# First expert gather of a layer from a contiguous copy of h, and new holds of the weight ring

## The chip, the cores and the metric

The kernel runs on one core of a Trainium2 chip. The metric is the device time of one execution in microseconds, the median of several runs. TensorE (PE; its weight loads are listed apart, as PEld), VectorE (DVE), ScalarE (ACT), GpSimd (POOL) and SyncE (SP, which issues the weight DMAs) run side by side and wait for each other by semaphores.

## The reference

Two layers of a decoder trunk over 256 tokens with 1024 features, in float32. Layer 0 mixes tokens by a gated short convolution and stick-breaking attention (the even mixer), layer 1 by a chunked gMLP (the odd mixer). After the mixer each layer has a mixture of experts: a router picks one of four groups and two of the group's eight experts for each token. Then comes a gate with a per-layer embedding, and a final norm.

```python
for i in range(DEPTH):
    xn = rmsnorm(h, norm_mix[i])
    h = h + (even_mixer if i % 2 == 0 else odd_mixer)(xn, ...)
    xn = rmsnorm(h, norm_ffn[i])
    h = h + hier_moe(xn, router_c[i], ..., moe_w1[i], moe_w3[i], moe_w2[i])
    gate = jax.nn.sigmoid(rmsnorm(h, norm_pl[i]) @ w_pg[i])
    h = h + gate * (p[i] @ w_pe[i])
return rmsnorm(h, final_norm)
# hier_moe, for each expert e of 32, width 256:
#   y += comb[:, e] * ((silu(xt @ w1[e]) * (xt @ w3[e])) @ w2[e])
```

## The kernel before, in words

**Storage.** h lies in SBUF with the tokens on the partitions: `h[P, 2, 1024]`, two tiles of 128 tokens. The view `hk` takes feature p*8+k as [k, p], so that `hk[:, tt, k, :]` is 128 features that lie eight floats apart; the experts' weights are loaded with the same order of features (`(p k) n -> p k n`), which gives long pieces in DRAM.

**The ring.** All large tiles and all weights share one pool of 25 buffers of one megabyte (`rawp`, `big`). `emit_loads` (L107) issues the next weight load while the live raw loads, two for each split unit, one for the load itself, one spare and `pos["hold"]` fit into 25. `HOLD` and `MOE_HOLD` are lists of holds, set at fixed places of the program, and keep room for the other large tiles of that stage. Weights are loaded in the order of use, by SP alone; a load is queued on SP in program order and waits there until the last reader of its buffer is done.

**The order of work.** It is written out by hand. In `odd_mixer` (L680) eight output units are interleaved with the projections and the gates (`gate`, L717): gate i+1 comes ahead of output unit i. `finish_mixer` (L463) does the last output unit, adds to h, turns h by TensorE into `hT` (L458), and computes the router's logits (L473) and 40 small matmuls on a tile of ones (L498). `moe` (L785) ranks the logits on VectorE and makes from them the selection matrix `S` of the first group (L849). `gather` (L855) multiplies: for each of eight k, `hk[:, tt, k, :]` is the weight and S the moving operand, so that the tokens of each expert stand in columns (`xg`); the result leaves PSUM through VectorE (L866). The first gather of a layer takes 128 columns of the first group (four experts with 32 places each), in two calls of four k. Then, for each quarter of a group, `up` (L910) multiplies by w1 and w3 of four experts and gives back their four buffers (`drop_raw`, L187, which calls `emit_loads`), and `down` (L962) does the same with w2. The second half of the first group is gathered after the first quarter's up-projections, the further groups whole, after every second quarter.

**What the change touches.** The two lists of holds (L31, L32), the end of `finish_mixer`, the loop over the output units in `odd_mixer` (L746 to L757), the weight operand of `gather` (L863), the place after the first two gathers (L872), and what hands the new tile through (L675, L758, L785, L1253 to L1287).

Of the kernel before, what the change touches and what calls it, by code (L numbers as in the profile page):

```python
# [15 lines left out]
P = 128  # L16
T = 256
D = 1024
KD = 8
# [8 lines left out]
NEG = -1.0e30  # L28
BUFS = 25
SPARE = 1  # L30
HOLD = (9, 2, 9, 8, 8, 6, 8)  # L31
MOE_HOLD = (0, 5, 10, 6, 1, 0)  # L32
UP_PIECES = 2
DOWN_PIECES = 2
MIX_PIECES = 1
# [11 lines left out]
def body(tc, x, p, norm_mix, norm_ffn, norm_pl, final_norm,  # L47
# [4 lines left out]
    nc = tc.nc  # L52
# [11 lines left out]
    def psum(name, tag="mm", dt=F32):  # L64
        n = 1024 if tag == "y" else 512
        return pp.tile([P, n], dt, name=name, tag=tag)

    def big(name, shape, dt=F32):
        return rawp.tile(shape, dt, name=name, tag="raw")
# [26 lines left out]
    pos = {"load": 0, "split": 0, "take": 0, "hold": HOLD[0]}  # L96
# [168 lines left out]
    h = cp.tile([P, 2, D], F32, name="h")  # L265
# [190 lines left out]
    def turn_plain(tt, n, hT):  # L456
        tv = turned(tt, n)
        nc.scalar.copy(hT[:, 4 * n:4 * n + 4, tt * P:(tt + 1) * P], tv)  # L458


    hk = h.rearrange("t a (p k) -> t a k p", k=KD)

    def finish_mixer(li, ops, ys, nxt, wr):  # L463

        pos["hold"] = MOE_HOLD[0]
        g = cols[:, FFN_C + 8 * li:FFN_C + 8 * li + 8].unsqueeze(2).to_broadcast([P, KD, 36])
        nc.vector.tensor_tensor(wr, wr, g, op=ALU.mult)
        hT = big("hT", [P, KD, T])
        lps = psum("lps", "mm")

        def logits(tt, n):
            for k in range(4 * n, 4 * n + 4):
                nc.tensor.matmul(lps[:, tt * 64:tt * 64 + 36], hT[:, k, tt * P:(tt + 1) * P],  # L473
                                 wr[:, k, :], start=(tt == 0 and k == 0), stop=True,
                                 skip_group_check=True)

        def after(tt, n):
            add_h(ops[tt][:, n * 512:(n + 1) * 512], tt, n)
            if n == 0 or tt == 0:
                nxt.square(tt, n)  # L480
            if (tt, n) == (0, 1):
                turn_plain(0, 0, hT)
                turn_plain(1, 0, hT)
        out_acc(ops, ys, False, True, after)
        done.clear()
        pos["hold"] = MOE_HOLD[5]
        emit_loads()
        turn_plain(0, 1, hT)
        nxt.square(1, 1)
        nxt.rstd()  # L490
        logits(0, 0)
        turn_plain(1, 1, hT)
        logits(1, 0)
        logits(0, 1)
        logits(1, 1)
        wps = psum("wps", "tp")
        for _ in range(GAP_WARM):
            nc.tensor.matmul(wps[:, 0:P], ones_b, ones_b, start=True, stop=True)  # L498
        return lps

    def bt(a):
        return a.unsqueeze(1).to_broadcast([P, 2, T])
# [2 lines left out]
    def even_mixer(norm, late_loads):  # L505
# [23 lines left out]
        for k in range(KD):  # L529
# [5 lines left out]
            if k == KD - 2:  # L535
                r = norm.rstd()
# [5 lines left out]
        ps = proj_cols(xH, xL, first=True)  # L542
# [127 lines left out]
        nxt = Norm()  # L670
        for i, kt in enumerate(EVEN_ORDER):
            ys = [(yH[:, kt + j, :], yL[:, kt + j, :]) for j in range(2)]
            if i < 3:
                out_acc(ops, ys, i == 0, False, more=i == 2)
            if i == 3:  # L675
                lps = finish_mixer(0, ops, ys, nxt, late["r"][0])
        return nxt, lps


    def odd_mixer(norm, xH, xL, w_sT, b_bc, make_w_sT, wr, hook):  # L680
        rb = None
        pos["hold"] = HOLD[6]
        v = [big("v0", [P, 4, 512]), big("v1", [P, 4, 512])]
        ssp = small("ssp", [P, 2, 4])
        for b in range(4):
            pss = proj_rows(xH, xL, ("mm", "y")[b % 2], hook=hook if b == 0 else None)
            if b == 0:
                r = norm.rstd()
            if b == 1:
                rb = norm.rows()  # L690
            if b == 2:
                make_w_sT()
            for tt in range(2):
                nc.scalar.activation(v[tt][:, b, :], pss[tt], AF.Gelu_apprx_tanh,
                                     scale=r[:, tt:tt + 1])
                sq = act("junk", [P, 512], BF16)
                nc.vector.scalar_tensor_tensor(sq, v[tt][:, b, :], 1.0 / 2048, v[tt][:, b, :],
                                               op0=ALU.mult, op1=ALU.mult,
                                               accum_out=ssp[:, tt, b:b + 1])
        ug = big("ug", [P, 2, 2, 2, T])  # L700
        yb = big("yb", [P, 2, 2, 2, T], F32R)

        def proj_u(n):
            ups = proj_cols(xH, xL)
            u, gt = ug[:, n % 2, 0], ug[:, n % 2, 1]
            nc.vector.tensor_tensor(u, ups, bt(rb), op=ALU.mult)
            nc.scalar.activation(u, u, AF.Gelu_apprx_tanh)
            return u, gt

        ss = small("ssv", [P, 2, 2])  # L710
        nc.vector.tensor_tensor(ss, ssp[:, :, 0:2], ssp[:, :, 2:4], op=ALU.add)
        rv = small("rv", [P, 2])
        rstd_of(rv, ss[:, :, 0], ss[:, :, 1])
        wms = big("wms", [P, 2, 8, P])
        for c in range(2):
            nc.vector.tensor_scalar(wms[:, c], w_sT, rv[:, c:c + 1], None, op0=ALU.mult)
        def gate(i, u):  # L717

            u, gt = u
            gps = psum("gps", "tp").rearrange("p (j t) -> p j t", t=T)  # L720
            for j in range(2):
                dt = 2 * i + j
                for c in range(2):
                    vs = slice((dt % 4) * P, (dt % 4) * P + P)
                    nc.tensor.matmul(gps[:, j, c * P:(c + 1) * P], v[c][:, dt // 4, vs],  # L725
                                     wms[:, c, i, :], start=True, stop=True)
            for j in range(2):
                dt = 2 * i + j
                bb = b_bc[:, i, :].unsqueeze(1).to_broadcast([P, 2, P])
                nc.vector.scalar_tensor_tensor(  # L730
                    gt[:, j, :].rearrange("p (c t) -> p c t", t=P),
                    gps[:, j, :].rearrange("p (c t) -> p c t", t=P),
                    cols[:, gv_c + dt:gv_c + 1 + dt], bb, op0=ALU.mult, op1=ALU.add)
            nc.vector.tensor_tensor(gt, gt, u, op=ALU.mult)
            yH, yL = yb[:, i % 2, 0], yb[:, i % 2, 1]
            nc.scalar.copy(yH, gt)
            nc.vector.tensor_tensor(yL, gt, f(yH), op=ALU.subtract)
            return [(yH[:, j, :], yL[:, j, :]) for j in range(2)]

        u = proj_u(0)  # L740
        ys = gate(0, u)
        u = proj_u(1)
        ops = [psum("ops", "y") for _ in range(2)]
        pos["hold"] = HOLD[3]
        nxt = Norm()
        for i in range(8):  # L746
            ys_next = gate(i + 1, u) if i < 7 else None
            if i < 7:
                out_acc(ops, ys, i == 0, False, more=i == 6)
            else:  # L750
                lps = finish_mixer(1, ops, ys, nxt, wr)
            if i < 6:
                u = proj_u(i + 2)
            if i == 5:
                pos["hold"] = HOLD[5]
                emit_loads()
            ys = ys_next  # L757
        return nxt, lps  # L758


    def turn_p(ptok):
# [20 lines left out]
        nc.scalar.copy(pe[:, tt, n * 512:(n + 1) * 512], ps)  # L782


    def moe(li, norm, lps, br):  # L785


        r = norm.r
# [66 lines left out]
        def gather(g, k0, n, tag, c0=0, c1=256):  # L855

            if k0 == 0 and c0 == 0:
                xg[g] = big("xg", [P, KD, 256])
            m = c1 - c0
            ps = psum("gat", tag)[:, 0:n * m].rearrange("p (k t) -> p k t", t=m)  # L860
            for tt in range(2):
                for k in range(n):
                    nc.tensor.matmul(ps[:, k], hk[:, tt, k0 + k, :], S[g][:, tt, c0:c1],  # L863
                                     start=(tt == 0 and k * m % 512 == 0), stop=True,
                                     skip_group_check=True)
            nc.vector.tensor_tensor(xg[g][:, k0:k0 + n, c0:c1], ps,  # L866
                                    gffn[:, li, k0:k0 + n].unsqueeze(2).to_broadcast([P, n, m]),
                                    op=ALU.mult)

        select(0)  # L870
        gather(0, 0, 4, "y", 0, P)
        gather(0, 4, 4, "y", 0, P)  # L872

        mc, m1 = small("mc", [P, 2]), small("m1", [P, 2])
        nc.vector.tensor_reduce(mc, lc, axis=AX.X, op=ALU.max)
# [374 lines left out]
    def late_loads():  # L1250
        late["r"] = router_operands(0)

    norm, lps = even_mixer(Norm(), late_loads)  # L1253
    pe, norm, pxH, pxL, rest = moe(0, norm, lps, late["r"][1])
    xT = {}

    def turn_next(tt, n):
# [25 lines left out]
        for t in range(2):  # L1283
            turn_next(t, 1)

    norm, lps = odd_mixer(norm, xT["h"], xT["l"], w_sT, b_bc, make_w_sT, wr, hook)
    pe, norm, pxH, pxL, rest = moe(1, norm, lps, br)  # L1287
    per_layer(norm, pe, pxH, pxL, rest)
    ctx.close()

# [24 lines left out]
```

## Time and profile before

| what | us |
|---|---|
| three runs | 748.73, 746.76, 748.25 |
| median | 748.25 |
| the profiled execution | 747.56 |
| its span, first to last instruction | 745.7 |

Engines over the span: PE 668.4 us (90%), PEld 496.9 (67%), DVE 289.1 (39%), ACT 225.6 (30%), POOL 20.2 (3%). DMA moved 259.18 MB, 348 GB/s on the mean. The mean granted clock of TensorE was 0.962 of full speed.

A busy share over the whole span says little here, because the stages differ: in some the weight DMAs run without a break, in others TensorE does. The slices of the page show which is which. In the chain that ended last, "DMA raw<-in_moe_w_dram" has 38% of the span and TensorE 47%.

### The profile page before, as it was taken

The page shows a single profiled execution, that of the slowest core. Times are in us where ns is not written, and L with a number is a line of the kernel's source. Part 1 is how long each engine was busy: PE and PEld are TensorE (multiplying, and loading weights), DVE is VectorE, ACT ScalarE, POOL GpSimd, SP SyncE. Part 2 cuts the span into 40 slices and gives each one's busy share as a digit, 9 for nine tenths or more (in the row PEclk, how much of TensorE's full clock was granted, in tenths as well). Part 3 has the DMA queues.
Part 4 walks back from the last instruction along what each step waited for, and adds up shares of the span by engine and source line. Part 5 has one row for each costly group of instructions (what it writes and reads, how often), then busy time and mean ns, then how long its engine had stood idle before and what let it go on. Part 6 is the DMA issues. An engine that isn't in the chain of part 4 may idle for free.

```text
span 745.7 us, 12322 instructions
## 1 busy us (share of the span) xinstructions
PE 668.4 (90%) x5268; PEld 496.9 (67%) x5268; DVE 289.1 (39%) x482; ACT 225.6 (30%) x334; POOL 20.2 (3%) x37
## 2 busy tenths in 40 slices
PE   8999998988898787699999999999998887877695
PEld 7989988755466453258789999987664554633265
DVE  6748733211112120057667765634121230110076
ACT  6446622111103010057544443431001122010084
POOL 3100000000000000001100000000000000000000
PEclk9999999999999898899999999999999999898998
DMA  9994599699999999999971545499999999999931
GB/s 317 374 420 174 174 425 427 278 425 427 426 425 427 425 426 425 426 409 402 382 266 57 177 170 204 149 418 412 419 427 427 425 425 426 427 426 424 420 135 57
DMA packets 61164, 259.18 MB, mean 348 GB/s; under 512 B 4309, under 2 KB 22897, under 8 KB 36273
## 3 DMA queue, kind: packets, MB, share of 16 engines
q1 hardware_dynamic: 60032, 255.87, 85.0%
q0 software_dynamic: 1072, 2.47, 0.9%
q8 instruction: 43, 0.70, 0.3%
q14 instruction: 17, 0.13, 0.0%
HBM read 257.28 MB, written 1.05 MB: 346 GB/s over the span
## 4 chain that ended last, share of the span: by engine, by line
PE 47%; DMA 41%; DVE 4%; issue 3%; ACT 2%; POOL 1%; SPq 0%; POOLq 0%; ACTq 0%; DVEq 0%
DMA raw<-in_moe_w_dram 38%; PE pc L417 14%; PE ops L260 9%; PE pr L260 6%; PE gat L863 5%; PE hps L919 5%; DMA raw<-in_w_pe_dram 3%; PE yps L972 2%; DVE wl L139 1%; PE gps L725 1%; PE tp L382 1%; PE lps L473 1%; DMA raw<-in_w_in_even_dram 1%; PE acc L1113 1%; ACT wh L130 1%
## 5 line engine op out<-in xcount | busy, mean ns | idle before, releaser
L919 PE MATMUL hps<-raw,xg 128*32 128x256 f32 x2048 | 142.3, 415 | 38.6 <-DMA raw<-in_moe_w_dram 23.1
L919 PEld LDWEIGHTS hps<-raw,xg 128*32 128x32 f32 x2048 | 69.8, 119 | 111.0 <-DMA raw<-in_moe_w_dram 31.5
L142 DVE TENSOR_TENSOR wl<-raw,wh 128x2048 fp32r<-128x2048 f32 (+1 forms) x45 | 95.7, 2147 | 16.6 <-ACT wh L132 15.2
L972 PE MATMUL yps<-raw,gHL 128*32 128x512 f32 x512 | 64.6, 610 | 22.1 <-ACT gHL L959 17.7
L863 PE MATMUL gat<-S,h 128*128 128x256 f32 (+1 forms) x320 | 78.6, 407 | 1.5 <-DVE S L849 1.5
L863 PEld LDWEIGHTS gat<-S,h 128*128 128x128 f32 x320 | 77.4, 336 | 2.8 <-DVE S L849 1.8
L132 ACT CAST wh<-raw 128x2048 fp32r<-128x2048 f32 (+1 forms) x41 | 74.1, 1826 | 13.2 <-DMA raw<-in_w_in_even_dram 7.2
L940 ACT CAST ST<-sl 128x256 fp32r<-128x256 f32 x16 | 6.0, 372 | 226.5 <-DVE gjunk L936 224.6
L972 PEld LDWEIGHTS yps<-raw,gHL 128*32 128x32 f32 x512 | 16.6, 111 | 58.7 <-issue 29.6
L983 DVE SCALAR_TENSOR_TENSOR o<-yps,gts,o 128x512 fp32r<-128x512 f32 x28 | 20.1, 748 | 83.3 <-ACT o L982 82.6
L866 DVE TENSOR_TENSOR xg<-gat,gffn 128x512 f32<-128x512 f32 x32 | 22.1, 692 | 66.0 <-PE gat L863 62.0
L417 PE MATMUL pc<-xTH,wh 128*128 128x256 f32 x288 | 42.3, 292 | 1.8 <-DVE wh L134 1.8
L260 PE MATMUL pr<-wh,xTH 128*128 128x512 f32 (+1 forms) x152 | 40.7, 390 | 1.4 <-ACT xTH L394 1.3
L417 PEld LDWEIGHTS pc<-xTH,wh 128*128 128x128 f32 x288 | 38.8, 198 | 2.8 <-ACT xTH L524 2.0
L417 PE MATMUL pc<-xTL,wh 128*128 128x256 f32 x288 | 40.3, 283 | 0.0
L417 PE MATMUL pc<-xTH,wl 128*128 128x256 f32 x288 | 40.3, 283 | 0.0
L260 PE MATMUL pr<-wl,xTH 128*128 128x512 f32 (+1 forms) x152 | 39.6, 382 | 0.4 <-DVE wl L142 0.4
L950 DVE TENSOR_TENSOR he<-sl,hps 128x256 f32<-128x256 f32 x16 | 6.7, 421 | 84.1 <-PE hps L919 84.1
L260 PE MATMUL pr<-wh,xTL 128*128 128x512 f32 (+1 forms) x152 | 39.0, 379 | 0.0
L417 PEld LDWEIGHTS pc<-xTL,wh 128*128 128x128 f32 x288 | 37.2, 192 | 0.0
L417 PEld LDWEIGHTS pc<-xTH,wl 128*128 128x128 f32 x288 | 37.1, 192 | 0.0
L982 ACT ACTIVATE o<-yps,gts 128x512 fp32r<-128x512 f32 x28 | 18.1, 684 | 58.1 <-PE yps L972 58.1
(225 smaller groups left out, 785.1 us busy)
## 6 DMA issues: line engine op xcount, KB each, us to landing
raw<-in_moe_w_dram SPq DMA_DIRECT2D x192, 1024.0 KB, 19.5
raw<-in_w_in_odd_dram SPq DMA_DIRECT2D x16, 1024.0 KB, 13.3
raw<-in_w_in_even_dram SPq DMA_DIRECT2D x11, 1024.0 KB, 11.8
raw<-in_w_pg_dram SPq DMA_DIRECT2D x8, 1024.0 KB, 12.6
raw<-in_w_out_odd_dram SPq DMA_DIRECT2D x8, 1024.0 KB, 6.7
raw<-in_w_out_even_dram SPq DMA_DIRECT2D x4, 1024.0 KB, 11.9
raw<-in_w_pe_dram SPq DMA_DIRECT2D x2, 1024.0 KB, 20.2
h<-in_x_dram SPq DMA_DIRECT2D x2, 512.0 KB, 4.3
```

The source lines that it names most:

```text
L130: nc.scalar.activation(wh[:, c], raw[:, c], AF.Copy, scale=cols[:, col + j:col + j + 1])
L132: nc.scalar.copy(wh[:, c], raw[:, c])
L139: nc.vector.scalar_tensor_tensor(wl[:, c], raw[:, c], cols[:, col + j:col + j + 1], f(wh[:, c]), op0=ALU.mult, op1=ALU.subtract)
L142: nc.vector.tensor_tensor(wl[:, c], raw[:, c], f(wh[:, c]), op=ALU.subtract)
L260: nc.tensor.matmul(ps, x, w, start=start and i == 0, stop=stop and i == 3 * n - 1)
L417: nc.tensor.matmul(o, w, xx, start=st, stop=True if first else i % (3 * KD) == 3 * KD - 1, skip_group_check=first)
L863: nc.tensor.matmul(ps[:, k], hk[:, tt, k0 + k, :], S[g][:, tt, c0:c1], start=(tt == 0 and k * m % 512 == 0), stop=True, skip_group_check=True)
L866: nc.vector.tensor_tensor(xg[g][:, k0:k0 + n, c0:c1], ps, gffn[:, li, k0:k0 + n].unsqueeze(2).to_broadcast([P, n, m]), op=ALU.mult)
L919: nc.tensor.matmul(ps[e * CAP:(e + 1) * CAP, :], x[:, k, c:c + CAP], ts[e][:, k, :], start=(k == 0), stop=(k == KD - 1))
L972: nc.tensor.matmul(ps[s, :], gs[:, j, s], ts[e][:, j, c], start=(j == 0), stop=(j == 1))
L982: nc.scalar.activation(o[:, 0, c], ps, AF.Copy, scale=gt[:, 0:1])
L983: nc.vector.scalar_tensor_tensor(o[:, 1, c], ps, gt[:, 0:1], f(o[:, 0, c]), op0=ALU.mult, op1=ALU.subtract)
```

## The change

`finish_mixer` copies h into a tile `xc` of the ring, [tt, k, p], in two ScalarE copies that follow the last turn copy; there the 128 features of one k are neighbours. The first two gather calls of a layer (group 0, columns 0 to 127) take their weight from `xc`, all others from `hk` as before. The holds from the mixer's last output unit on are one larger, for `xc`; after these two gathers the hold is 0 and loads are issued. In the odd mixer the hold falls from 6 to 2 behind the last gate (i = 6), where loads are issued too.

```diff
-HOLD = (9, 2, 9, 8, 8, 6, 8)
-MOE_HOLD = (0, 5, 10, 6, 1, 0)
+HOLD = (9, 2, 9, 8, 8, 6, 8, 2)
+MOE_HOLD = (1, 5, 10, 6, 1, 1, 0)
...
         nxt.rstd()
         logits(0, 0)
         turn_plain(1, 1, hT)
+        xc = big("xc", [P, 2, KD, P])
+        for tt in range(2):
+            nc.scalar.copy(xc[:, tt], hk[:, tt])
         logits(1, 0)
         logits(0, 1)
         logits(1, 1)
...
-        return lps
+        return lps, xc
...
             ys_next = gate(i + 1, u) if i < 7 else None
+            if i == 6:
+                pos["hold"] = HOLD[7]
+                emit_loads()
             if i < 7:
                 out_acc(ops, ys, i == 0, False, more=i == 6)
...
-    def moe(li, norm, lps, br):
+    def moe(li, norm, lps, xc, br):
...
             m = c1 - c0
+
+            src = xc if g == 0 and c0 == 0 else hk
             ps = psum("gat", tag)[:, 0:n * m].rearrange("p (k t) -> p k t", t=m)
             for tt in range(2):
                 for k in range(n):
-                    nc.tensor.matmul(ps[:, k], hk[:, tt, k0 + k, :], S[g][:, tt, c0:c1],
+                    nc.tensor.matmul(ps[:, k], src[:, tt, k0 + k, :], S[g][:, tt, c0:c1],
...
         select(0)
         gather(0, 0, 4, "y", 0, P)
         gather(0, 4, 4, "y", 0, P)
+        pos["hold"] = MOE_HOLD[6]
+        emit_loads()
```

## Rows read from the trace of the kernel before

**Rows 1.** The page: GB/s in 40 equal slices of the span.

```profile
GB/s 317 374 420 174 174 425 427 278 425 427 426 425 427 425 426 425 426 409 402 382 266 57 177 170 204 149 418 412 419 427 427 425 425 426 427 426 424 420 135 57
```

**Rows 2.** Chain of waits, 100 to 180: start us, us, what.

```profile
124.03 0.44 DVE S L849
124.52 7.91 PE gat L863 x32
132.43 3.59 PE hps L919 x64
...
140.42 7.84 PE gat L863 x32
```

**Rows 3.** Windows, 131 to 138: engines' busy us (x count), clock, DMA share, GB/s.

```profile
131.00:132.00 1.00, 1.00 (x5) 1.00 (x6) 0.00 (x0) 0.00 (x0) 0.00 (x0) 1.00 0.18 74
...
136.00:137.00 1.00, 1.00 (x13) 0.75 (x14) 0.15 (x3) 0.00 (x0) 0.00 (x0) 1.00 0.00 0
137.00:138.00 1.00, 1.00 (x24) 0.65 (x20) 0.11 (x3) 0.75 (x2) 0.00 (x0) 1.00 0.80 156
```

**Rows 4.** SP's waits, 126 to 138, then 504 to 522: us, times, longest.

```profile
SPq L115 <- PE hps L919: 19.8, 1, 19.8
...
SPq L115 <- PE hps L919: 14.7, 1, 14.7
```

**Rows 5.** Windows of 10 us, first and last of 140 to 320.

```profile
140.00:150.00 10.00, 10.00 (x76) 8.84 (x72) 1.80 (x3) 0.00 (x0) 0.00 (x0) 1.00 1.01 425
...
310.00:320.00 10.00, 8.86 (x68) 4.61 (x68) 0.42 (x1) 0.04 (x1) 0.00 (x0) 0.66 1.01 419
```

**Rows 6.** Chain of waits, 310 to 330.

```profile
311.01 6.58 PE hps L919 x58
...
320.39 4.07 PE yps L972 x31
```

**Rows 7.** Tile yps, 316 to 326: its engine idle before it (us, times), until.

```profile
  DMA raw<-in_moe_w_dram: 0.3, 1
```

**Rows 8.** Chain of waits, 480 to 545.

```profile
486.88 0.89 PE gps L725 x8
...
508.68 7.92 PE gat L863 x32
```

**Rows 9.** Groups by line and form, 480 to 520: busy us, mean ns | idle.

```profile
L863 PEld LDWEIGHTS gat<-S,h 128*128 128x128 f32 x32 | 7.7, 336 | 0.9 <-DVE S L849 0.9
...
L725 PEld LDWEIGHTS gps<-wms,v 128*128 128x128 f32 x8 | 1.0, 192 | 0.0
```

**Rows 10.** Windows in which the granted clock (third from the right) moves.

```profile
120.00:130.00 10.00, 8.26 (x70) 8.04 (x70) 4.49 (x17) 0.00 (x0) 0.00 (x0) 0.83 1.01 424
125.00:126.00 1.00, 1.00 (x6) 1.00 (x6) 0.00 (x0) 0.00 (x0) 0.00 (x0) 0.92 0.99 418
...
312.00:313.00 1.00, 1.00 (x16) 0.44 (x12) 0.00 (x0) 0.00 (x0) 0.00 (x0) 0.50 1.01 426
...
511.00:512.00 1.00, 1.00 (x6) 1.00 (x6) 0.00 (x0) 0.00 (x0) 0.00 (x0) 0.77 1.03 434
```

**Rows 11.** Windows around the first gather of the second layer.

```profile
486.00:521.00 35.00, 33.05 (x263) 28.58 (x265) 13.75 (x47) 9.38 (x19) 0.69 (x1) 0.95 1.01 421
521.00:525.00 4.00, 4.00 (x67) 2.39 (x67) 0.43 (x4) 0.75 (x2) 0.00 (x0) 1.00 0.95 338
525.00:545.00 20.00, 17.14 (x164) 12.00 (x167) 3.26 (x8) 2.27 (x5) 0.00 (x0) 1.00 1.01 426
```

**Rows 12.** Line L132, ScalarE copies: ns min/median/max, first and last start, forms.

```profile
L132 ACT CAST wh<-raw x41: 1074/1907/1922, 12.9 to 610.3; 128x2048 fp32r<-128x2048 f32 x37, 128x1024 fp32r<-128x1024 f32 x4
```

**Rows 13.** Instructions in time, layer 0; in brackets the idle time before.

```profile
133.46 0.21 ACT L879 ACTIVATE ec<-ec 128x8 f32<-128x8 f32 x1 [15.23 <-DVE ec L878]
```

**Rows 14.** Instructions in time, layer 1.

```profile
490.23 0.69 DVE L737 TENSOR_TENSOR yb<-ug,yb 128x512 fp32r<-128x512 f32 x1 [0.74 <-ACT yb L736]
...
517.63 0.21 ACT L879 ACTIVATE ec<-ec 128x8 f32<-128x8 f32 x1 [13.94 <-DVE ec L878]
```

More of the change, by code (lines that the diff above doesn't have):

```diff
@@ L675, in even_mixer @@
             if i == 3:
-                lps = finish_mixer(0, ops, ys, nxt, late["r"][0])
-        return nxt, lps
+                lps, xc = finish_mixer(0, ops, ys, nxt, late["r"][0])
+        return nxt, lps, xc
     def odd_mixer(norm, xH, xL, w_sT, b_bc, make_w_sT, wr, hook):
@@ L750, in odd_mixer @@
             else:
-                lps = finish_mixer(1, ops, ys, nxt, wr)
+                lps, xc = finish_mixer(1, ops, ys, nxt, wr)
             if i < 6:
@@ L757, in odd_mixer @@
             ys = ys_next
-        return nxt, lps
+        return nxt, lps, xc
     def turn_p(ptok):
@@ L1251, in late_loads @@
         late["r"] = router_operands(0)
-    norm, lps = even_mixer(Norm(), late_loads)
-    pe, norm, pxH, pxL, rest = moe(0, norm, lps, late["r"][1])
+    norm, lps, xc = even_mixer(Norm(), late_loads)
+    pe, norm, pxH, pxL, rest = moe(0, norm, lps, xc, late["r"][1])
     xT = {}
@@ L1284, in hook @@
             turn_next(t, 1)
-    norm, lps = odd_mixer(norm, xT["h"], xT["l"], w_sT, b_bc, make_w_sT, wr, hook)
-    pe, norm, pxH, pxL, rest = moe(1, norm, lps, br)
+    norm, lps, xc = odd_mixer(norm, xT["h"], xT["l"], w_sT, b_bc, make_w_sT, wr, hook)
+    pe, norm, pxH, pxL, rest = moe(1, norm, lps, xc, br)
     per_layer(norm, pe, pxH, pxL, rest)
```

## The prediction

> **What bounds the kernel now.** I read the page's row of GB/s by slices first, for what is full where; then the chain of waits around the start of each expert layer; then SP's own waits and the microsecond windows there, to see when the stream of weights stops and what starts it again. The slices [rows 1] show two kinds of stretch. At 425 to 428 GB/s the weight stream is full, and no faster engine can shorten the stretch. Where it falls (slices 4 and 5, slice 8, slices 21 to 26) the ring of 25 buffers is full and SP waits for an engine to free one, so engine time counts there.
>
> Slice 8 is the start of the first expert layer. The chain [rows 2] runs from the selection matrix S over the first gather (32 passes, 7.91 us) to the first up-projection (64 passes, 3.59 us), whose end at 136.02 frees four weight buffers. The windows [rows 3] show the stream running dry at 131.2 and back at 137.2, with nothing moved between; SP stood 19.8 us waiting for the L919 matmul [rows 4]. From there it is full until the layer's last weights: the 18 ten-us windows from 140 to 320 carry 419 to 428 GB/s, of which the first and the last stand there [rows 5]. The last weights and the hidden turn meet at the last down-projection at 320.39 [rows 6]; it still lost 0.3 us to a weight DMA [rows 7]. So the layer's end lies a fixed number of bytes behind the moment at which the stream comes back, and that moment lies behind the gather. After it come per-layer gate and odd mixer, where TensorE works through and all that follows shifts with it.
>
> The second expert layer looks the same in the chain (gather 7.92 us from 508.68) [rows 8], but there the stream is already full before it. SP waited 14.7 us for L919 [rows 4], yet with loads enough still on the way only 521 to 525 runs at 338 GB/s, against 426 after it [rows 11].
>
> **The change, part by part.** *The gather from xc.* Same 32 passes, same S, same PSUM target; only the weight operand differs: each weight load reads 128 neighbouring floats instead of floats eight apart. Rows of the same form (128*128, 128 columns, f32) stand side by side [rows 9]: the gather's load takes 336 ns, the odd gate's (neighbouring floats) 192. The pace is what counts: 7.91/32 = 247 ns a pass for the gather [rows 2], 0.89/8 = 111 ns for the gate [rows 8]. I take 111 ns, the same form to the last figure: 32 x 0.111 = 3.56 us, 4.35 us less per layer. The bounds are 0 (the load stays at 247 ns whatever the layout) and 4.35.
>
> *The clock.* In the gather TensorE's granted clock fell from 2.4 to 1.2 GHz (0.50), behind a pause in which TensorE had little but waited for VectorE's selection: in layer 0 at 125.84 (mean 0.92 in 125 to 126, so 0.16 us at 0.50) and for 3.4 us (mean 0.83 in 120 to 130) [rows 10]. The strided gather did not care: its second half, from 140.42 at a clock of 1.00 [rows 5], took 7.84 us against 7.91 [rows 2], so the strided load sets its pace. A dense pass will care: the up-projection ran 58 passes in 6.58 us at 0.50 [rows 6, 10], 113 ns each, against 3.59/64 = 56 ns [rows 2], twice as long. If the clock falls again at 125.84, 1.32 us hold 12 passes, 3.4 us at 222 ns hold 15, the last 5 take 0.56: 5.3 us, a gain of 2.6 instead of 4.35.
>
> *The copy.* Two ScalarE copies of 128x1024 with a read step of 32 bytes are added to each layer. A plain one of that size takes 1.07 us (the smallest of L132) [rows 12]. Strided reads on ScalarE do not occur in the trace. Low bound 1.07 each; high, by the stretch of the weight load's pace (247/111), 2.4 each. ScalarE has been idle for 15.23 us when it goes on at 133.46, so from 118.23 [rows 13]; S is ready, and the gather starts, at 124.52. So 2.1 to 4.8 us lie in a cover of 6.3 us: cost 0 (in layer 1 it is idle from 503.69 at the latest, 13.94 before 517.63 [rows 14], and the gather starts at 508.68 [rows 8]). If the cover were gone, each microsecond beyond it would delay the gather by one. The page Advanced Engine Details and Errata of the Trainium skill (SBUF Cachelines) says that accesses that each touch another 16-byte line are penalised; it names no price. That rule would explain the 336 against 192 ns, and it moves the penalty from TensorE to the copy, so it speaks against the edit where the copy isn't covered; by the rows it is.
>
> *The ring.* xc takes one of the 25 buffers, so by the new holds the last load before the gather is issued behind the gather instead of at the mixer's end, into xc's own buffer. In layer 0 this load (one megabyte, 2.46 us at 426 GB/s) goes into the hole: the gather ends at 128.08, data come about 1.2 us after the release (136.02 to 137.2 [rows 2, 3]), so from 129.3 to 131.8; the stream without it is full to about 131.2 - 2.5 = 128.7. The next release, the end of the up-projection, comes at 131.67 and its data at 132.9. So the load is done before: cost 0. It waits at the head of SP's queue with all later weights behind it, but these wait for later matmuls anyway. Were the gather not shorter (132.43), the load would run from 133.6 to 136.1, still inside the old hole: also 0. In layer 1 the gather would end at 512.2; the load before the gap at 521 has to start 2.5 us ahead of it, at 518.7, so a release at 512.2 plus 1.2 is in time.
>
> *The odd gates.* Four loads are issued after the last gate instead of one output unit later in program order. The stream is then already full (421 GB/s on the mean of 486 to 521 [rows 11]). Gain 0, at most the (426 - 421)/426 x 35 = 0.4 us that this stretch lacks. The risk is a buffer that is freed late: the last reader of the gate's tile is the VectorE subtract at 490.23, 0.69 us [rows 14]; data from there would come at 492.1, about when the load ahead is through. Cost 0, at most 1.0 (the whole of one such release latency).
>
> **Sum.** Layer 0: release at 131.67 instead of 136.02, so the stream and all behind it come 4.35 us sooner. Layer 1: the stream lacks (426 - 338)/426 x 4 us = 0.83 us in 521 to 525; a release 4.35 us sooner closes that and no more, because the stream is full on both sides. Together 5.2 us. The profiled execution took 747.56 us (span 745.7 and 1.86 around it), hence 742.4; the runs' median is 748.25, 0.7 above the profiled one, so I forecast 748.25 - 5.2 = 743.1. What is late next: in layer 0 the weight stream again, in the hole as well as after it; before the gather it is VectorE's selection, which ends with S at 124.47.
>
> **Rivals.**
> 1. *The clock eats a part.* The gather in layer 0 takes 5.3 us: gain 2.6 + 0.83 = 3.4, 744.8. For it: in both layers the clock fell inside this gather and what TensorE does ahead of it stays. Against it: it fell 1.3 us after the gather's start in layer 0 and 2.9 us after it in layer 1 (mean 0.77 in 511 to 512, so at 511.54) [rows 8, 10], behind the same work, so the point isn't tied to the work, and a gather of 3.56 us is over, or nearly so, at the later one. In layer 1 the fall costs nothing, since 0.83 us is all there is to win. With the low clock over the whole gather (32 x 0.222 = 7.1 us) the gain is 0.8 + 0.8 and the time 746.6. The Trainium skill's page TensorE: Matmul & The Clock Gate (Part 1: The HAM clock gate) says that the activity monitor runs free of the kernel's start; the two different points agree, and by that rule the fall in layer 0 is a matter of chance in each run.
> 2. *The layout isn't what is slow.* If the load costs 336 ns because of h itself or of the 32-pass group, the gather stays at 7.9 us, the held load disappears in the hole, and the time is 748.2, no change. Against it: the gate's form is equal in all but the layout.
> 3. *Slower: the copy outlasts its cover.* One mechanism: ScalarE's strided read. From 6.3 us for the pair it delays the gather; from 6.3 + 4.35 = 10.7 us, 5.3 us a copy, five times the plain one, layer 0 is slower than before. At 6.5 us a copy the gather would start 6.7 us late and end 2.4 us late: 748.25 + 2.4 = 750.6, and layer 1's hole grows too. For it: no row has such a read. Against it: TensorE pays 2.2 times for it, not five.
> 4. *A load of the odd gates stalls.* The buffers change hands in another order; up to 1.0 us of stream is lost at 490, so 743.1 + 1.0 = 744.1.
>
> **How the numbers follow.** Chances: forecast 0.55, rival 1 0.22, rival 2 0.10, rival 3 0.05, rival 4 0.08. The forecast's own range is 741.1 to 744.1: its low end is the fastest run of before less the sum and the 0.4 us of the odd gates (746.76 - 5.2 - 0.4), its high end rival 4. Rival 1 reaches from 744.8 to 746.6. The range 741.1 to 746.6 holds these and leaves out rivals 2 and 3, 0.15. About 0.3%, 2.2 us, is what a measurement of this kernel can tell from no change: faster is below 746.0. Forecast, rival 4 and nearly all of rival 1 are that: 0.82. Rival 2 and the rest of 1 make 0.12 for the same, rival 3 with the runs that scatter past 750.5 0.06 for slower.
>
> **What would show it.** The gather's 32 passes from xc at 111 ns (3.6 us; weight loads at 192 ns), or about 5.3 us with a granted clock of 0.50 inside; two copies on ScalarE over by 123; no idle DMA window longer than about 1.5 us between 128 and 134, and the stream full from 133; everything behind it 4.3 us earlier up to the odd mixer; no window under 400 GB/s between 505 and 530. It is wrong if the gather still takes over 6 us, if it waits for ScalarE, or if the stream loses the time again before the layer's last weights.

## The result, and the profile after

The changed kernel took 743.92 us (median of 8 runs, 742.87 to 745.28) against 747.88 (8 runs, 746.57 to 749.06): 0.9949 of the time before, interval 0.9938 to 0.9961, so 4.0 us less. The forecast was 743.1, the range 741.1 to 746.6, the forecast gain 5.2 us. Two later series of the same kernel gave 0.9942 and 0.9938. The profiled execution took 744.45 us (span 742.6) against 747.56.

The page's GB/s by slices of the changed kernel, to be laid beside [rows 1]:

```profile
GB/s 322 372 420 162 177 424 401 361 425 427 425 425 428 425 427 425 425 408 401 382 252 54 187 166 208 147 418 425 427 425 424 427 426 426 426 427 424 420 133 57
```

Slice 8 (the eighth number) still has a dent, 361 where it had 278, and slice 7 has a new small one, 401 for 425, since the stream now runs dry earlier, at 129; the slices of the second layer's start (28 to 30) are full. The instructions in time around the first gather of layer 0 (start us, us, engine, line; in brackets the idle time before and who ended it), once from the timeline of all engines:

```profile
118.10 4.01 ACT L495 COPY xc<-h 128x1024 f32<-128x1024 f32 x2
...
124.01 0.76 DVE L855 TENSOR_TENSOR S<-place,slots 128x256 f32<-128x256 f32 x2
124.58 5.44 PE L871 MATMUL gat<-S,xc 128*128 128x128 f32 x32 [0.86 <-DVE S L855]
130.08 0.33 SPq L115 DMA_DIRECT2D raw<-in_moe_w_dram  x1
```

The copies end at 122.1; the gather starts at 124.58 behind S, as before. It takes 5.44 us instead of 7.91 [rows 2], not 3.56: the windows of one us there (PE, weight loads, VectorE, ScalarE, GpSimd; granted clock, DMA share, GB/s) show the clock at 0.75 on the mean of 125 to 126, 0.50 to 128, and 1.00 from 129. Behind the gather they show how much of the hole [rows 3] is left:

```profile
125.00:126.00 1.00, 1.00 (x9) 1.00 (x8) 0.00 (x0) 0.00 (x0) 0.00 (x0) 0.75 0.97 410
...
127.00:128.00 1.00, 1.00 (x7) 1.00 (x6) 0.40 (x1) 0.00 (x0) 0.00 (x0) 0.50 1.01 426
128.00:129.00 1.00, 1.00 (x7) 1.00 (x7) 0.29 (x1) 0.00 (x0) 0.00 (x0) 0.55 0.74 311
129.00:130.00 1.00, 1.00 (x13) 0.88 (x16) 0.00 (x0) 0.00 (x0) 0.00 (x0) 1.00 0.12 49
130.00:131.00 1.00, 1.00 (x21) 0.62 (x24) 0.95 (x5) 0.00 (x0) 0.00 (x0) 1.00 0.00 0
131.00:132.00 1.00, 1.00 (x27) 0.61 (x20) 0.64 (x6) 0.94 (x3) 0.00 (x0) 1.00 0.66 147
132.00:133.00 1.00, 1.00 (x26) 0.57 (x22) 0.86 (x7) 0.86 (x2) 0.00 (x0) 1.00 0.98 418
133.00:134.00 1.00, 1.00 (x16) 0.59 (x9) 0.57 (x5) 0.00 (x0) 0.00 (x0) 1.00 1.00 426
134.00:135.00 1.00, 1.00 (x16) 0.60 (x19) 0.24 (x3) 0.23 (x1) 0.00 (x0) 1.00 0.78 156
135.00:136.00 1.00, 1.00 (x24) 0.64 (x20) 0.00 (x0) 0.52 (x2) 0.00 (x0) 1.00 0.69 246
```

The held load goes out at 130.08, its data fill 131.4 to 134, and the four buffers of the up-projection follow. SP's long waits in 126 to 138 are one of 14.2 us for the gather and one of 3.3 for the up-projection, in place of one of 19.8 [rows 4]:

```profile
SPq L115 <- PE gat L871: 14.2, 1, 14.2
SPq L115 <- PE hps L929: 3.3, 1, 3.3
```

Layer 1 met the full clock. Its groups by line and form, 480 to 520 (busy us, mean ns), against [rows 9], and two windows against [rows 11]:

```profile
L871 PE MATMUL gat<-S,xc 128*128 128x128 f32 x32 | 3.8, 277 | 0.9 <-DVE S L855 0.9
...
L871 PEld LDWEIGHTS gat<-S,xc 128*128 128x128 f32 x32 | 3.6, 192 | 0.9 <-issue 0.9
...
L871 PEld LDWEIGHTS gat<-S,h 128*128 128x128 f32 x10 | 2.5, 333 | 0.4 <-issue 0.4
```

```profile
519.00:523.00 4.00, 4.00 (x19) 4.00 (x18) 0.69 (x1) 0.00 (x0) 0.00 (x0) 1.00 1.01 426
523.00:543.00 20.00, 17.14 (x191) 10.59 (x191) 3.43 (x9) 2.28 (x5) 0.00 (x0) 1.00 1.01 427
```

32 passes in 3.81 us, weight loads at 192 ns where those from h take 333, and the 338 GB/s gap is gone.

**Where the 3.1 us between the two profiled executions come from.** The last down-projection of layer 0 is a good mark, since the stream of weights sets it. Lines of its tile yps, 280 to 360 (ns min/median/max, first and last start), of the kernel before and then of the changed one:

```profile
L972 PE MATMUL yps<-raw,gHL x64: 592/592/617, 297.2 to 323.9; 128*32 128x512 f32 x64
```

```profile
L982 PE MATMUL yps<-raw,gHL x64: 592/592/617, 296.6 to 321.6; 128*32 128x512 f32 x64
```

From the gather's start to the last start of yps it was 199.4 us (124.52 to 323.9) in the kernel before and is 197.0 (124.58 to 321.6) in the changed one: -2.4. From there to the gather of layer 1: 184.8 (to 508.68) and 184.5 (to 506.11): -0.3, which is the scatter of other work (below). From that gather to the end of the span: 237.0 and 236.5: -0.5. The gather of layer 0 starts 0.1 later. Sum -3.1.

### The profile page after: what moved, and what is told of

It reads as the page before. It is cut to its first block, busy times and chain, and to the rows that moved or that the text cites. A ratio compares the mean times of both kernels' runs of the same rounds, so it can differ in the third digit from the quotient of the medians.

```text
span 742.6 us, 12330 instructions
## 1 busy us (share of the span) xinstructions
PE 662.9 (89%) x5268; PEld 491.0 (66%) x5268; DVE 289.0 (39%) x482; ACT 233.6 (31%) x338; POOL 20.2 (3%) x37
## 3 DMA queue, kind: packets, MB, share of 16 engines
HBM read 257.28 MB, written 1.05 MB: 348 GB/s over the span
## 4 chain that ended last, share of the span: by engine, by line
PE 36%; DMA 15%; DVE 4%; issue 3%; ACT 3%; POOL 1%; POOLq 0%; ACTq 0%; DVEq 0%; SPq 0%
DMA raw<-in_moe_w_dram 15%; PE pc L417 6%; PE hps L929 6%; PE ops L260 6%; PE pr L260 5%; PE gat L871 5%; PE yps L982 3%; DVE wl L139 1%; PE gps L728 1%; PE acc L1123 1%; PE acc L1000 1%; PE peps L260 1%; PE tp L382 1%; PE acc L1002 1%; ACT wh L130 1%
## 5 line engine op out<-in xcount | busy, mean ns | idle before, releaser
L132 ACT CAST wh<-raw 128x2048 fp32r<-128x2048 f32 (+1 forms) x41 | 74.1, 1827 | 13.8 <-DMA raw<-in_w_in_even_dram 8.1
L871 PE MATMUL gat<-S,h 128*128 128x256 f32 (+1 forms) x256 | 62.8, 403 | 0.0
L871 PEld LDWEIGHTS gat<-S,h 128*128 128x128 f32 x256 | 62.0, 336 | 1.1 <-issue 0.8
```

Of the source, the lines that this page charges most:

```text
L132: nc.scalar.copy(wh[:, c], raw[:, c])
L871: nc.tensor.matmul(ps[:, k], src[:, tt, k0 + k, :], S[g][:, tt, c0:c1], start=(tt == 0 and k * m % 512 == 0), stop=True, skip_group_check= ...
```

## The experiments

All share one theory and two rivals. Theory: the gather's weight layout makes the gain, one for one through the stream of layer 0, and what is missing of it is the low clock inside the dense gather. Rivals: the gain comes from somewhere else (another buffer, the odd gates' earlier loads); or the rest is missing for a reason other than the clock.

**The changed kernel again** (no edit).

> The changed kernel once more, as the measure for the others of this group. Theory (the weight load's layout set the gather's pace; the gain is the earlier release of four weight buffers, less what the low clock takes in the first layer): ratio to the kernel before 0.993 to 0.996, gather of layer 1 at 3.8 us, that of layer 0 between 3.8 us (clock 1.00) and 5.4 us (clock 0.50 for most of it), whichever this execution meets. If the fall of the clock in layer 0 is tied to the pause before the gather, it is there again.

743.96 us (742.18 to 745.34, 6 runs), 0.9942 (0.9926 to 0.9958). The profiled execution met the other case. TensorE in time:

```profile
125.26 3.81 PE L871 MATMUL gat<-S,xc 128*128 128x128 f32 x32 [0.86 <-DVE S L855]
...
505.11 5.44 PE L871 MATMUL gat<-S,xc 128*128 128x128 f32 x32 [0.86 <-DVE S L855]
```

```profile
L982 PE MATMUL yps<-raw,gHL x64: 592/592/617, 294.6 to 320.5; 128*32 128x512 f32 x64
```

Full clock in layer 0, 0.50 in layer 1. From the gather of layer 0 to the last down-projection it is 195.2 us, 4.1 less than before. In layer 1 the slower gather costs nothing: from its start to the end of the span 236.5 us, as with 3.81.

**TensorE kept busy up to the gather**: more matmuls of ones ahead of the ranking and ten behind it.

```
-GAP_WARM = 40
+GAP_WARM = 54
...
+        wps = psum("wps", "tp")
+        for _ in range(10):
+            nc.tensor.matmul(wps[:, 0:P], ones_b, ones_b, start=True, stop=True)
```

> The changed kernel with TensorE kept at work through the pause before the gather: 54 instead of 40 matmuls on ones ahead of the ranking, and 10 more behind the ranking's matmuls. Theory (the rest of the forecast gain was taken by the low clock): no window at 0.50 inside the gather of layer 0, gather 3.8 us there instead of 5.4, buffers released 1.6 us sooner, time 1.2 to 1.7 us under the changed kernel where that meets the low clock, ratio 0.992 to 0.994. Rival (the low clock is not what took it, or the extra matmuls delay the gather): no difference from the changed kernel, 0.995.

743.28 us (741.92 to 745.02, 6 runs), 0.9937 (0.9922 to 0.9953). Both gathers took 3.81 us; 195.35 us from the gather to the last down-projection. The gain over the changed kernel is within the scatter.

```profile
119.48 3.18 PE L501 MATMUL wps<-ones_b 128*128 128x128 bf16 x54
122.85 0.18 PE L840 MATMUL rps<-Mb,upper_b 128*128 128x32 bf16 x1 [0.19 <-DVE Mb L832]
...
124.05 3.81 PE L874 MATMUL gat<-S,xc 128*128 128x128 f32 x32 [0.30 <-DVE S L858]
```

**Without the odd gates' earlier loads.**

```
-            if i == 6:
-                pos["hold"] = HOLD[7]
-                emit_loads()
```

> The changed kernel without the part at the odd gates (no hold of 2 and no loads behind the last gate). Theory: that part does nothing, because the loads concerned are released by the same instructions and the stream is already full; time within 0.5 us of the changed kernel, issues at the same places. Rival: part of the second layer's gain of 0.9 us comes from it; 0.5 to 1 us more than the changed kernel.

743.93 us (742.52 to 747.84, 9 runs), 0.9947 (0.993 to 0.9964): the time of the changed kernel. That part is worth nothing that can be measured, and the gain doesn't come from it.

**The copy in h's own order**, so that the gather reads another buffer, but strided as before.

```
-            nc.scalar.copy(xc[:, tt], hk[:, tt])
+            nc.scalar.copy(xc[:, tt].rearrange("t k p -> t (k p)"), h[:, tt])
...
-        return lps, xc
+        return lps, xc.rearrange("t a k p -> t a (k p)").rearrange("t a (p k) -> t a k p", k=KD)
```

> The changed kernel with xc copied in h's own order, so that the gather reads from xc floats that lie eight apart, as it did from h: tile, copies and holds stay, only the layout is undone. Theory: gather back at 7.9 us in both layers, copies at 1.1 us each instead of 2.05, time as the kernel before, ratio 0.998 to 1.002. Rival (h itself, shared with other readers, was slow, or the ring's new order brought the gain): gather at 3.8 to 5.4 us or ratio at 0.995.

747.99 us (746.42 to 750.5, 12 runs), 1.0005 (0.9993 to 1.0018): all of the gain is gone, with the copy, the holds and the ring as in the changed kernel. Groups by line and form, 116 to 140:

```profile
L871 PE MATMUL gat<-S,xc 128*128 128x128 f32 x32 | 7.9, 423 | 0.9 <-DVE S L855 0.9
...
L871 PEld LDWEIGHTS gat<-S,xc 128*128 128x128 f32 x32 | 7.7, 336 | 0.9 <-issue 0.9
...
L495 ACT COPY xc<-h 128x1024 f32<-128x1024 f32 x2 | 2.0, 1047 | 0.0
```

The clock fell inside this gather too (at 124.4) and it still took 7.9 us. The plain copy takes 1047 ns; the strided one of the changed kernel 2054.

**The second half gathered from xc as well**, and xc's buffer kept until then.

```
-            src = xc if g == 0 and c0 == 0 else hk
+            src = xc if g == 0 else hk
...
-        pos["hold"] = MOE_HOLD[6]
-        emit_loads()
...
-        pos["hold"] = MOE_HOLD[4]
+        pos["hold"] = MOE_HOLD[4] + 1
...
                 gather(0, 4, 4, "y", P, 2 * P)
+                pos["hold"] = MOE_HOLD[4]
+                emit_loads()
```

> The changed kernel with the second half of the first group's gather taken from xc too; xc is held until then, so the load that was issued behind the first gather goes out with the release of the first up-projection. Theory (engine time counts only where the ring is full and the stream stands): the second gather falls from 7.85 to about 3.9 us in both layers, 4 us less of TensorE each, and that gives nothing, while the held load's 2.4 us move out of the hole into the full stretch of layer 0; time 1.5 to 2.5 us over the changed kernel, about 745.5 to 746.5. Rival (TensorE's chain counts there too): 4 us less per layer against 2.4 us, time 739 to 742.

746.12 us (744.95 to 746.76, 5 runs), 0.9962 (0.9942 to 0.9982): 2.2 us over the changed kernel, although the second gather fell from 7.92 to 3.84 us. The load that would have gone out behind the first gather waits, and the hole is empty again:

```profile
131.00:132.00 1.00, 1.00 (x24) 0.65 (x20) 0.63 (x5) 0.97 (x3) 0.00 (x0) 1.00 0.00 0
...
133.00:134.00 1.00, 1.00 (x17) 0.59 (x10) 0.54 (x5) 0.00 (x0) 0.00 (x0) 1.00 0.00 0
134.00:135.00 1.00, 1.00 (x19) 0.58 (x23) 0.24 (x3) 0.27 (x1) 0.00 (x0) 1.00 0.96 139
```

4 us of TensorE time where the stream is full are worth nothing; one megabyte less in the hole (2.46 us at 426 GB/s) costs 2.2 by time and 2.5 in the trace (table below).

**Both copies made twice**, so that ScalarE's cover runs out.

```
-            for tt in range(2):
-                nc.scalar.copy(xc[:, tt], hk[:, tt])
+            for _ in range(2):
+                for tt in range(2):
+                    nc.scalar.copy(xc[:, tt], hk[:, tt])
```

> The changed kernel with the two copies made twice: 8.2 us of ScalarE where the cover before the gather is 6 us. Theory (the copies cost nothing because they are covered, and beyond the cover each microsecond delays the gather): ScalarE is done near 126.3 instead of 122.2, the gather of layer 0 ends 0.8 to 1.8 us later, time 0.8 to 1.8 us over the changed kernel; layer 1 has room and pays nothing. Rival (another step hides the copies or delays the gather): no difference, or the full 4 us.

745.12 us (743.55 to 746.79, 4 runs), 0.994 (0.9919 to 0.9961). By time that can't be told from the changed kernel (1.2 us more, on four runs). The trace shows the wait; weight loads of the gather:

```profile
125.11 0.97 PEld L872 LDWEIGHTS gat<-S,xc 128*128 128x128 f32 x8 [0.94 <-ACT xc L496]
126.61 4.35 PEld L872 LDWEIGHTS gat<-S,xc 128*128 128x128 f32 x24 [0.54 <-ACT xc L496]
```

The first 8 passes need the first copied half alone; the weight loads of the others wait 0.54 us for ScalarE, less than the 0.8 us expected at least. The gather ends 6.0 us after its start (126.61 + 4.54 - 125.14, the passes of the second part taking 4.54, partly at the low clock).

**The same busy TensorE on the kernel before** (the edit of the second experiment).

> The kernel before with the same extra matmuls in the pause as in e2_fill. Theory (the strided load sets the gather's pace at either clock): gather still 7.9 us whether or not the clock falls, time as the kernel before, ratio 0.998 to 1.002. Rival (the low clock was a cost of the kernel before as well): ratio 0.994 to 0.997.

748.59 us (747.25 to 751.85, 10 runs), 0.9999 (0.9985 to 1.0013). The strided gather is the same whatever TensorE does ahead of it, here at a granted clock of 1.00 from start to end, in the kernel before with 3.4 us at 0.50 inside:

```profile
L866 PE MATMUL gat<-S,h 128*128 128x128 f32 x32 | 7.9, 406 | 0.2 <-DVE S L852 0.2
```

**TensorE left idle ahead of the gather.**

```
-GAP_WARM = 40
+GAP_WARM = 1
```

> The changed kernel with 1 instead of 40 matmuls on ones, so that TensorE stands still for over 4 us ahead of the gather in both layers. Theory (the clock decides what a dense gather takes): granted clock 0.50 over most of the gather of layer 0 in this execution, gather 5.3 to 7.1 us, time 1 to 3 us over the changed kernel (744.8 to 747). Rival (the gather's time does not hang on the clock): as the changed kernel.

747.35 us (744.69 to 748.65, 10 runs), 0.9976 (0.9961 to 0.999): 3.4 us over the changed kernel. The clock is at 0.50 when the gather starts at 125.77 and comes back to 1.00 at 131.16, 1.0 us before its end; windows of one us and the group in 120 to 136:

```profile
122.00:123.00 1.00, 0.00 (x0) 0.00 (x0) 0.86 (x5) 1.00 (x1) 0.00 (x0) 0.50 0.99 418
...
130.00:131.00 1.00, 1.00 (x6) 1.00 (x6) 0.31 (x1) 0.00 (x0) 0.00 (x0) 0.50 0.06 25
131.00:132.00 1.00, 1.00 (x10) 0.96 (x8) 0.00 (x0) 0.00 (x0) 0.00 (x0) 0.92 0.00 0
```

```profile
L871 PE MATMUL gat<-S,xc 128*128 128x128 f32 x32 | 6.4, 391 | 0.9 <-DVE S L855 0.9
```

Some 7 of the 32 passes fall into that last 1.0 us, so about 25 took 5.4 us, 0.22 us each, twice the pace at the full clock. By that a dense gather wholly at 1.2 GHz would take about 7.1 us (an estimate; no execution here has one), still less than the strided one's 7.9. TensorE stood still for 3.09 us ahead of the ranking, not for over 4. The fall itself, at 120.92, came before the place where the 39 matmuls are missing (the one that is left starts at 121.17), so they can't have brought it; what sets this execution apart is that the clock was then low for 10.2 us, and that both first gathers started at 0.50 (the second at 508.39, after a fall at 506.63 in the pause). In all other executions here they started at 1.00. That the matmuls of ones keep the gather fast is thus likely, but one execution doesn't show it.

Against the changed kernel's first execution the gather starts 1.2 us later, the stretch from it to the last down-projection is 1.0 longer (198.0 against 197.0), and that from the gather of layer 1, 6.22 us here, to the end 1.3 (237.8 against 236.5). Only the 1.0 is the gather's. The changed kernel's own executions start the gather at 124.58, 125.26 and 126.91; and in layer 1 the kernel before, with a gather of 7.92 us, has 237.0 to the end. Where the 1.3, and most of the 3.4 us by time, come from is open.

**Again the changed kernel, and again the busy TensorE, without and with the odd gates' part taken out** (the edits of the second and third experiment).

> The changed kernel for the third time, beside the filled pause. Theory: ratio to the kernel before 0.994 to 0.995; the executions fall into ones with a gather of 3.8 us and ones of 5.4 us in layer 0, so the median lies about 0.8 us above that of the filled pause.

> The filled pause once more. Theory: clock at 1.00 through both gathers, 3.8 us each, ratio 0.992 to 0.994, 0.5 to 1.5 us under the changed kernel. Rival: no difference beyond 0.3 us, the low clock is not what the forecast lacks.

> The filled pause without the part at the odd gates. Theory: as the filled pause within 0.5 us, ratio 0.992 to 0.994. Rival: the part at the odd gates is worth 0.5 us or more.

743.82 us (743.57 to 747.1, 5 runs), 743.67 (742.54 to 745.51, 6) and 743.95 (742.75 to 745.27, 6); ratios 0.9938, 0.9938 and 0.9935. By time the rival holds: with TensorE busy it is 0.15 us less and 0.13 more than the changed kernel beside it, not 0.5 to 1.5 less. The changed kernel's profiled execution had the low clock in both gathers (5.44 us each). The two busy ones had gathers of 3.81, but in both the clock fell earlier, in the added matmuls. For the first of them the windows of one us, then TensorE:

```profile
118.00:119.00 1.00, 1.00 (x9) 1.00 (x9) 0.00 (x0) 1.00 (x2) 0.00 (x0) 0.68 1.00 426
...
120.00:121.00 1.00, 1.00 (x12) 1.00 (x10) 0.83 (x6) 0.83 (x1) 0.00 (x0) 0.50 1.05 442
```

```profile
119.09 4.46 PE L501 MATMUL wps<-ones_b 128*128 128x128 bf16 x54
123.39 0.18 PE L840 MATMUL rps<-Mb,upper_b 128*128 128x32 bf16 x1
```

54 of them take 4.46 us instead of 3.18, and the ranking queues behind them: VectorE waited 1.18 us for it instead of 0.32, so the gather starts 0.9 us late. So this execution gives back half of the 1.6 us that the full clock is worth.

**The ten matmuls behind the ranking alone.**

```
+        wps = psum("wps", "tp")
+        for _ in range(10):
+            nc.tensor.matmul(wps[:, 0:P], ones_b, ones_b, start=True, stop=True)
```

> The changed kernel with 10 more matmuls of ones directly behind the ranking's matmuls, and none added ahead of it, so nothing can hold the ranking up. Theory of the clock (the low clock inside the first gather takes the rest of the gain): with TensorE busy for about 0.6 us of the pause behind the ranking, the gather of layer 0 takes 3.8 us and the median is about 743.0, some 0.9 us under the changed kernel's 743.9; the wait of VectorE for the ranking (0.3 to 1.3 us in the kernels with both fills) stays near the 1.0 us or less of the changed kernel. Rival (where the clock falls does not depend on these ten matmuls): the gather takes 5.4 us in some executions as it does without them, and the median is 743.9. A difference under about 0.5 us can't be told here.

744.51 us (742.82 to 745.1, 6 runs), 0.995 (0.9936 to 0.9963): no gain, as the rival said for the time. The trace does as the theory said: both gathers 3.81 us, no wait of the ranking.

```profile
123.45 0.18 PE L840 MATMUL rps<-Mb,upper_b 128*128 128x32 bf16 x1 [0.96 <-DVE Mb L832]
...
124.64 3.81 PE L874 MATMUL gat<-S,xc 128*128 128x128 f32 x32 [0.30 <-DVE S L858]
```

The last down-projection lies at 320.0, 195.4 us behind the gather and 1.6 ahead of the changed kernel's first execution; at the odd mixer's start 0.9 of that is lost. There ScalarE waits for rstd, the factor of the norm, which GpSimd computes. ScalarE in time, of this kernel:

```profile
366.44 1.27 ACT L697 ACTIVATE v<-pr,rstd 128x512 f32<-128x512 f32 x2 [4.00 <-POOL rstd L376]
```

The changed kernel's first execution has 3.15 at this place. The difference stands on GpSimd: its second pause between two issues (last section) is 6.43 us here and 5.49 there.

**All profiled executions together.** Length of the first gather of layer 0, and the time from its start to the start of the last down-projection (us; for the copies made twice the length has the wait in it):

```
kernel                       gather   to the last yps
before                        7.91        199.4
busy TensorE, before          7.92        199.4
copy in h's own order         7.88        199.4
TensorE idle                  6.38        198.0
copies twice                  6.0         197.5
changed, 1st                  5.44        197.0
changed, 3rd                  5.44        197.0
changed, 2nd                  3.81        195.2
without odd gates' part       3.81        195.2
busy TensorE (4 kernels)      3.81        195.3 to 195.4
both halves from xc           5.44        199.5
```

But for the last line, the right column less the gather's length lies between 191.4 and 191.7 everywhere: layer 0 ends a fixed time behind the end of this gather, whatever made the gather long or short. In the last line it is 194.0, because there the load that fills the hole is held back: 2.5 us more.

## Why the prediction came out as it did

*The gather's pace.* The pace was right, the sum a little short: forecast 111 ns a pass and 3.56 us, measured 3.81 us at the full clock. In this line of the second busy kernel's trace, cut off at 128, 31 of the passes take 3.70 us; all 32 take 3.81, so a pass more costs 0.11 us, as forecast:

```profile
124.54 3.70 PE L874 MATMUL gat<-S,xc 128*128 128x128 f32 x31 [0.30 <-DVE S L858]
```

The 0.25 us left out is what a group takes beyond its passes times the pace, since one pass by itself lasts 277 ns. The 7.91 us of the strided gather hold such an end; the gate's 0.89 [rows 8], counted to the start of the next work, does not (its eight passes are busy for 1.1 us). So layer 0 wins 4.1 us there and not 4.35. Rival 2 (not the layout) fell with the copy in h's own order.

*Layer 1.* The mechanism was right (421, 338 and 426 GB/s [rows 11] became 426 and 427 there), the size too large: 0.5 of the forecast 0.83 reach the end, measured from the gather to the end of the span. Taken from the issue of the first load of that unbroken stream to the landing of the last, it is 0.88 (221.35, from 484.98 to 706.33, to 220.47, from 482.74); the two differ by where the gather stands in the stream, 23.70 and 23.37 us behind that issue. The difference is small beside the scatter: from this gather to the end the three executions with the strided gather have 236.9 to 237.0, nine with a dense one 236.4 to 236.7, but two others 237.5 (copies twice) and 237.8 (TensorE idle), for a reason that is open. With this the sum at full clock is 4.6 us, not 5.2. The second execution checks it by spans: 4.1 and 0.5, and 0.2 from the last down-projection to the next gather (184.6 against 184.8), less the 0.7 by which its first gather starts later, make 4.1; its span is 4.1 shorter (741.6 against 745.7).

*The clock.* The low clock was a rival with 0.22; the profiled execution met it, and its price was right: 5.44 us (forecast 5.3), 2.4 us won in layer 0 (2.6). Of five profiled executions with the copies and TensorE's work as in the changed kernel (three of this kernel, one without the odd gates' part, one with both halves from xc) three met it in the gather of layer 0 and two did not: it came in layer 0 alone, in layer 1 alone, or in both. The page TensorE: Matmul & The Clock Gate of the Trainium skill (Part 1: The HAM clock gate) says that the activity monitor runs free of the kernel's start; these executions agree. Three of five would take 1.0 us off the mean (3/5 of 1.63), leaving 3.6; the means of all runs, with their standard errors, are 748.21 +- 0.12 (70 runs) and 744.10 +- 0.25 (19 runs), 4.1 +- 0.3 apart, as if about three in ten met it. How often it does is open. With TensorE busy none of four did (in both layers, the clock fell in 6 of the 10 first gathers without it and in none of the 8 with it), but these kernels' 24 runs have a mean of 743.81 +- 0.20, 0.3 +- 0.3 less than the changed kernel's. So the low clock explains the difference between executions in the trace. Of the 1.1 us by which the gain falls short of 5.2, the two terms make 0.6; that the low clock makes the other 0.5 is likely, but by time it is not shown. The term that came out too large in the sum is "the release 4.35 us sooner": it is 4.1 at the full clock and 2.4 where the clock falls.

*Luck.* The time came out nearer than the gain: 743.92 against 743.1, but 4.0 us against 5.2. The forecast started from the median of three runs, 748.25, and that of eight was 747.88; these 0.4 us of the agreement are luck.

*The copy.* Cost 0 was right: 2.05 us each, within the bounds of 1.07 and 2.4 and nearer the high one, over at 122.1 where the gather starts at 124.58. The price of the stride moved from TensorE to ScalarE, where a copy takes 2054 ns strided and 1047 plain. The page Advanced Engine Details and Errata of the Trainium skill (SBUF Cachelines) says that accesses that each touch another line are penalised; the trace agrees. The cover is real and ends: with the copies doubled the gather's weight loads wait 0.54 us for them. Rival 3 would have needed 5.3 us a copy.

*The held load.* Right: out at 130.08, behind the gather, into the hole. It is free only there: in the kernel that gathers both halves from xc, where it misses the hole, it costs 2.2 us.

*The odd gates.* Cost 0, gain 0: right as far as the runs tell, by the kernel without that part (743.93 against 743.96 in the same series; about 1 us could be told).

*What was to show it.* "The stream full from 133" failed: 156 and 246 GB/s stand in 134 to 136. It isn't the low clock alone: the second busy kernel's gather starts at 124.54 and has the full clock, and 133 to 135 still run at 205 and 377. So at the full clock too the stream is full only from 135. "No window under 400 between 505 and 530" held but for one microsecond of 393 (422 on the mean of 484 to 519, 426 in 519 to 523, 427 after it).

## What to carry to other kernels

A matmul whose weight operand is read with a stride can be limited by that read: compare the weight loads of two rows of one form. Before making an engine faster, find the place where the ring is full and the stream stands, since 4 us there were worth 4 and 4 us beside a full stream nothing. A step that is made dense begins to depend on the clock that the strided form hid, so price it at both levels, and look at several executions before calling one number the gain.

## What the runs showed of the hardware that was not expected

- The strided gather takes 7.9 us for 32 passes at 2.4 GHz throughout (the kernel before with TensorE busy) and as much with 3.4 us at 0.50 inside (the kernel before). The dense one takes 3.81 at 2.4 GHz, 5.44 with such a fall 0.9 us after its start, and 6.4 with its first 5.4 us at 0.50: about 0.11 us a pass at one level and, as an estimate, 0.22 at the other.
- A ScalarE copy of 128x1024 floats takes 1.05 us plain and 2.05 with a read step of 32 bytes.
- GpSimd's issues of four small router loads stand on the path into the odd mixer, in every kernel here. The chain of waits of the changed kernel's second execution:

```profile
356.95 0.90 POOL wr L336
357.84 5.56 issue
363.40 0.89 POOL wr L337
...
364.83 0.55 POOL br L340
365.39 0.73 POOL rstd L376
```

"issue" is a pause that nothing in the profile explains. ScalarE waits 3.0 to 4.0 us for the rstd behind it (3.15 before). How much of this wait could be won is open: moving these issues behind the rstd was not tried.
